# Seven Strassen products for seven pairs of k tiles in each half of a down-projection

## The chip, the cores and the metric

The kernel runs on one core of a Trainium2 chip. Work is shared between TensorE (PE, matrix products), VectorE (DVE) and ScalarE (ACT, both elementwise), GpSimd (POOL, elementwise) and SyncE (SP, which here only starts DMA transfers). The metric is the device time of one execution in microseconds; the kernel before takes 1110.88 us (median of three runs, 1110.84 to 1110.97).

## The reference

One decoder layer on 256 tokens of width 2048. Attention and convolution come first, then the part that matters here, a gated MLP with a three-tap depthwise convolution over the tokens:

```
u = causal_depthwise_conv(rms_norm(x) @ w_up, cw, cb)     # 256 x 11264
a, gate = split(u)                                        # each 256 x 5632
x = x + (silu(gate) * a) @ w_down                         # w_down is 5632 x 2048
return rms_norm(x, final_norm_g)
```

All inputs are float32. TensorE multiplies in the reduced type fp32r, so every operand is split into a high part (a copy in fp32r) and a low part (the value minus its high part), and a product is three matmuls: high times high, high times low, low times high.

## The kernel before, in words

The order of the instructions on each engine is the order in which the program issues them. Weights come in chunks of 128 partitions x 2048 columns (1 MB). `w_dma` starts the transfer of a chunk into one of three raw buffers (`wraw`), `w_split` copies it to a high part `wh` on ScalarE (L110) and subtracts for the low part `wl` on VectorE (L115), three buffers each; the end of the subtraction starts the transfer of the chunk three later. `w_next` hands out a chunk and first splits the chunk two further on. So while TensorE works on chunk c, chunk c+2 is split, into the buffers that chunk c-1 has just left.

The up-projection (L1019, L1021) has 88 chunks. Each of its 22 steps `m` makes two k tiles of the gated activation `gt` (128 x 256 each). `up_out` puts the work behind it in three stages, `join`, `three_taps` and `gate`, and `up_stages` issues the next stage of each waiting step at every chunk. The last of these stages fall into the first chunks of the down-projection.

The down-projection has two halves `h` of 1024 output columns. Each half runs through 22 chunks, called pairs here because one holds two k tiles (256 rows of `w_down`, 1024 columns). For a pair, `down_chunk` multiplies two k tiles x two row blocks `t` (128 tokens) x two column blocks `n` (512 columns), eight products of three matmuls (`mm_rows`, L151 to L153), 24 in all, into four PSUM banks, one for each (t, n). The activations are split four k tiles at a time by `gsplit` (L954 on ScalarE, L955 on VectorE) into `gh` and `gl`, two buffers each, one step of two pairs ahead. The first half's four banks are added to the residual `x2` during the second half (`first_half`). The last two pairs of the second half run in `last_rows`, row block by row block, with the final norm and the output behind them.

Of the kernel before, what the change touches and what calls it, by code (L numbers as in the profile page):

```python
# [35 lines left out]
POOLED = (5, 32)  # L36

# [9 lines left out]
def hybrid_trunk(ctx: ExitStack, tc: tile.TileContext, a: dict, out: bass.AP):  # L47
# [29 lines left out]

    NR, NB, LA = 3, 3, 2
    st = {"dma": 2, "split": 2, "use": 0}
    raws, parts, pieces = {}, {}, []  # L80
    late = []
# [14 lines left out]

    def w_split(cuts):
# [4 lines left out]
        st["split"] += 1  # L102
        n = chunks[c][1]
# [22 lines left out]
    def w_next(cuts=1, ahead=LA):  # L126
        c = st["use"]
        st["use"] += 1
        w_pump()
        while st["split"] <= min(c + ahead, len(chunks) - 1):  # L130
            w_pump()
            w_split(cuts)
# [50 lines left out]
    def norm_evac(src, k, g):  # L183
        nc.scalar.activation(xt_h[:, k], src, AF.Copy, scale=g[:, k:k + 1])
        nc.vector.scalar_tensor_tensor(xt_l[:, k], src, g[:, k:k + 1], xt_h[:, k].bitcast(F32),
                                       op0=OP.mult, op1=OP.subtract)
# [4 lines left out]
    xt = mixp.tile([P, KD, 2, T], F32R, name="xt")  # L191
    xt_h, xt_l = xt[:, :, 0], xt[:, :, 1]
# [3 lines left out]
    with ExitStack() as mx:  # L196
# [40 lines left out]
        for (lo, hi), (xc, *wc) in zip(CUTS, heads):  # L237
            for k in range(lo, hi):
                xk = xc[:, (k - lo) * T:(k - lo + 1) * T]
                nc.scalar.activation(xt_h[:, k], xk, AF.Copy, scale=mix_g[:, k:k + 1])  # L240
                nc.vector.scalar_tensor_tensor(xt_l[:, k], xk, mix_g[:, k:k + 1], xt_h[:, k].bitcast(F32),
# [107 lines left out]
        def tile_chunk(ps, ticks={}):  # L349

            wh, wl = w_next(2)
            for kt in range(KD):
                if kt % 4 == 2:
                    hook(kt // 4, ticks)
                sl = slice(kt * P, (kt + 1) * P)
                mm3(ps, wh[:, sl], wl[:, sl], xt_h[:, kt], xt_l[:, kt], kt == 0, kt == KD - 1)
# [53 lines left out]
        for j in range(8):  # L410
            gb, ab = [b[:, :T] for b in bank[2 * (j if j < 3 else (j + 1) % 2):][:2]]
            if j == 0:
                pair = [w_next(2), w_next(2, 1)]
                for lo, hi in CUTS:
                    for ps, (wh, wl) in zip((gb, ab), pair):
                        for k in range(lo, hi):
                            sl = slice(k * P, (k + 1) * P)
                            mm3(ps, wh[:, sl], wl[:, sl], xt_h[:, k], xt_l[:, k], k == 0, k == KD - 1)
# [195 lines left out]
        for kh in range(2):  # L614
            wh, wl = [w.rearrange("p (k c) -> p k c", c=256) for w in w_next(2)]
            for k in range(8):
# [3 lines left out]
                for t in range(2):  # L620
                    sl = slice(t * P, (t + 1) * P)
                    o = vb[t][:, :256]
                    nc.tensor.matmul(o, xt_h[:, kt, sl], wh[:, k], start=kt == 0, stop=False)
                    nc.tensor.matmul(o, xt_h[:, kt, sl], wl[:, k], start=False, stop=False)
                    nc.tensor.matmul(o, xt_l[:, kt, sl], wh[:, k], start=False, stop=kt == KD - 1)
# [3 lines left out]
        for kq in range(4):  # L629
            wh, wl = [w[:, :4 * 304].rearrange("p (k c) -> p k c", c=304) for w in w_next(2)]  # L630
            for k in range(4):
                kt = kq * 4 + k
                hook(k)
                for t in range(2):
                    sl = slice(t * P, (t + 1) * P)
                    o = vb[t][:, :304]
                    nc.tensor.matmul(o, xt_h[:, kt, sl], wh[:, k], start=kt == 0, stop=False)  # L637
                    nc.tensor.matmul(o, xt_h[:, kt, sl], wl[:, k], start=False, stop=False)
                    nc.tensor.matmul(o, xt_l[:, kt, sl], wh[:, k], start=False, stop=kt == KD - 1)  # L639
# [294 lines left out]
    with ExitStack() as fx:  # L934
        fp = fx.enter_context(tc.tile_pool(name="fp", bufs=1))
        fw = fx.enter_context(tc.tile_pool(name="fw", bufs=2))
        gt = fp.tile([P, NFT, T], F32, name="gt")
# [4 lines left out]
        gq = []  # L942
        gn = {"n": 0}

        def gsplit():
# [3 lines left out]
            if n >= 2 * (NFT // 4):  # L949
                return  # L950
            src = gt[:, 4 * (n % (NFT // 4)):4 * (n % (NFT // 4)) + 4]
            gh = fw.tile([P, 4, T], F32R, name="gh", bufs=2)
            gl = fw.tile([P, 4, T], F32R, name="gl", bufs=2)
            nc.scalar.activation(gh, src, AF.Copy)  # L954
            nc.vector.tensor_sub(gl, src, gh.bitcast(F32))  # L955
            gq.append((gh, gl))

# [4 lines left out]
        def up_out(m, part, banks, ya):  # L962
# [3 lines left out]
            def join():  # L966
                for i in range(2):
                    u = fw.tile([P, T], F32, name="u", bufs=4)
# [5 lines left out]
            def three_taps():  # L974
                for i in range(2):
                    c = part * NFT + 2 * m + i
                    yt = fw.tile([P, T], F32, name="yt", bufs=8)
# [9 lines left out]
            def gate():  # L987
                for i in range(2):
                    nc.scalar.activation(ys[i], ys[i], AF.Silu)
                    nc.vector.tensor_mul(gt[:, 2 * m + i], ys[i], ya[i])  # L990
# [16 lines left out]
        for m in range(NFT // 2):  # L1007
            ya = {}
            if m == NFT // 2 - 1:
                gsplit()  # L1010
            for part in range(2):
                bk = UP_BANKS[2 * ((2 * m + part) % 4):][:2]
                for kh in range(2):
                    wh, wl = [w.rearrange("p (k c) -> p k c", c=256) for w in w_next(1 if m + part + kh else 2)]
                    up_stages()
                    for n, (k, i) in enumerate((k, i) for k in range(8) for i in range(2)):
                        kt = kh * 8 + k
                        sl = slice(i * P, (i + 1) * P)
                        nc.tensor.matmul(bk[i], wh[:, k, sl], xt[:, kt].rearrange("p a t -> p (a t)"),  # L1019
                                         start=kt == 0, stop=False)  # L1020
                        nc.tensor.matmul(bk[i][:, :T], wl[:, k, sl], xt_h[:, kt], start=False, stop=kt == KD - 1)  # L1021
# [9 lines left out]
        def down_chunk(ws, g, banks, k2, t):  # L1031
            sl = slice(t * P, (t + 1) * P)
            for k in range(2):
# [148 lines left out]
```

## Time and profile before

| | us |
|---|---|
| timed runs, median of three | 1110.88 |
| span of the profiled execution, first to last instruction | 1109.3 |
| time of the timed runs outside such a span | 1.6 |
| up-projection | about 363.5 to 853.4 |
| down-projection on TensorE | 853.5 to 1100.9 |
| from there to the end | 8.4 |

Times in the profile count from the first instruction. A row of the timeline gives start, duration, engine, line, operation, tile written and tiles read, count, and in brackets the idle time of the engine ahead of it and what ended it. PE is a matmul on TensorE and PEld a weight load. The end of a matmul in the profile is modelled and overlaps the next one, so the pace is read from starts. A row of a table by stage gives, for a stretch of time, the busy time and the number of instructions of each engine, the granted TensorE clock, the DMA share and GB/s.

### The profile page before, as it was taken

To read this page: it belongs to the slowest core of one execution; us is meant where nothing else is said; L and a number is where in the kernel's file an instruction comes from. 1 tells how busy PE (TensorE), PEld (TensorE's weight loads), DVE (VectorE), ACT (ScalarE), POOL (GpSimd) and SP (SyncE) were. 2 spreads that over 40 slices of the span, in tenths; PEclk is the share of its full clock that TensorE was granted. 3 is DMA by queue.
4 is the path that set the end of the run, shared out by engine and by line. 5 is a ranking of instruction groups with operands and counts; after the bars stand their busy time and mean duration, and the time that the engine had idled before them with its cause. 6 is when DMAs were issued, how large, how long until landed. Compare 5 with 4: busy or idle time off the path is not lost.

```text
span 1109.3 us, 16328 instructions
## 1 busy us (share of the span) xinstructions
PE 1096.5 (99%) x6530; PEld 957.0 (86%) x6530; DVE 768.5 (69%) x1255; ACT 574.3 (52%) x833; POOL 183.7 (17%) x143
## 2 busy tenths in 40 slices
PE   8999999999999999999999999999999999999997
PEld 8999999987788888888888888888888888888885
DVE  7899966776445777777777777777778555556554
ACT  7444456677645545554555455545555444444442
POOL 0878856657000000000000000000000000000000
PEclk9999999999999999999999999999999999999999
DMA  9685526222555555555555555555555555555542
GB/s 375 240 296 188 179 85 232 111 101 91 205 214 184 201 188 189 190 192 188 191 190 192 190 190 189 190 189 189 193 189 193 183 187 190 190 189 190 189 153 77
DMA packets 32425, 207.46 MB, mean 187 GB/s; under 512 B 3883, under 2 KB 6203, under 8 KB 8284
## 3 DMA queue, kind: packets, MB, share of 16 engines
q1 hardware_dynamic: 28972, 199.85, 50.0%
q10 hardware_dynamic: 3376, 6.55, 1.6%
q8 instruction: 51, 0.84, 0.3%
q14 instruction: 26, 0.21, 0.1%
HBM read 204.27 MB, written 2.12 MB: 186 GB/s over the span
## 4 chain that ended last, share of the span: by engine, by line
PE 94%; DVE 2%; ACT 1%; DMA 1%; issue 1%; POOL 0%; SPq 0%; DVEq 0%; POOLq 0%; ACTq 0%
PE bank L1019 29%; PE bank L1021 15%; PE bank L153 10%; PE bank L151 10%; PE bank L152 10%; PE bank L144 5%; PE bank L146 5%; PE bank L145 5%; PE bank L804 1%; PE bank L784 1%; DMA hb<-in_head 1%; DVE wl L115 1%; PE bank L533 0%; PE bank L639 0%; PE bank L637 0%
## 5 line engine op out<-in xcount | busy, mean ns | idle before, releaser
L110 ACT ACTIVATE wh<-wraw 128x2048 fp32r<-128x2048 f32 (+2 forms) x239 | 355.8, 1505 | 369.0 <-issue 153.0
L115 DVE TENSOR_TENSOR wl<-wraw,wh 128x2048 fp32r<-128x2048 f32 (+1 forms) x185 | 363.4, 1970 | 194.8 <-ACT wh L110 194.6
L1019 PE MATMUL bank<-xt,wh 128*128 128x512 f32 x1408 | 488.6, 394 | 0.0
L1021 PE MATMUL bank<-xt,wl 128*128 128x256 f32 x1408 | 390.0, 277 | 0.0
L1019 PEld LDWEIGHTS bank<-xt,wh 128*128 128x128 f32 x1408 | 264.0, 188 | 61.3
L1021 PEld LDWEIGHTS bank<-xt,wl 128*128 128x128 f32 x1408 | 264.2, 188 | 0.0
L144 PE MATMUL bank<-xt,wh 128*128 128x256 f32 x512 | 146.7, 287 | 1.9 <-ACT wh L245 1.9
L146 PE MATMUL bank<-xt,wl 128*128 128x256 f32 x512 | 145.1, 283 | 0.3 <-DVE wl L246 0.2
L145 PE MATMUL bank<-xt,wh 128*128 128x256 f32 x512 | 144.8, 283 | 0.0
L152 PE MATMUL bank<-wl,gh 128*128 128x512 f32 (+1 forms) x360 | 140.8, 391 | 0.0
L151 PE MATMUL bank<-wh,gh 128*128 128x512 f32 (+1 forms) x360 | 140.8, 391 | 0.0
L153 PE MATMUL bank<-wh,gl 128*128 128x512 f32 (+1 forms) x360 | 140.8, 391 | 0.0
L180 POOL TENSOR_TENSOR rstd<-ms,half 128x1 f32<-128x1 f32 x4 | 2.2, 554 | 821.7 <-DVE ms L173 821.7
L115 POOL TENSOR_TENSOR wl<-wraw,wh 128x1024 fp32r<-128x1024 f32 (+1 forms) x54 | 121.4, 2282 | 31.1 <-ACT wh L110 27.5
L144 PEld LDWEIGHTS bank<-xt,wh 128*128 128x128 f32 x512 | 97.7, 191 | 3.7 <-ACT wh L245 2.3
L146 PEld LDWEIGHTS bank<-xt,wl 128*128 128x128 f32 x512 | 97.8, 191 | 0.7 <-DVE wl L246 0.7
L145 PEld LDWEIGHTS bank<-xt,wh 128*128 128x128 f32 x512 | 97.8, 191 | 0.4
L376 DVE SCALAR_TENSOR_TENSOR bank<-us,cw,bank 128x256 f32<-128x256 f32 x232 | 93.9, 481 | 1.7 <-ACT bank L371 1.2
L982 DVE SCALAR_TENSOR_TENSOR yt<-u,vecs,yt 128x255 f32<-128x255 f32 (+1 forms) x176 | 80.9, 480 | 3.1
L151 PEld LDWEIGHTS bank<-wh,gh 128*128 128x128 f32 x360 | 67.8, 188 | 15.8
L153 PEld LDWEIGHTS bank<-wh,gl 128*128 128x128 f32 x360 | 67.8, 188 | 15.8
L152 PEld LDWEIGHTS bank<-wl,gh 128*128 128x128 f32 x360 | 67.8, 188 | 15.8
(182 smaller groups left out, 1030.8 us busy)
## 6 DMA issues: line engine op xcount, KB each, us to landing
wraw<-in_w_u SPq DMA_DIRECT2D x88, 1024.0 KB, 4.7
wraw<-in_w_d SPq DMA_DIRECT2D x44, 1024.0 KB, 4.7
wraw<-in_w_t SPq DMA_DIRECT2D x30, 1024.0 KB, 5.1
wraw<-in_w_o SPq DMA_DIRECT2D x16, 1024.0 KB, 4.8
wraw<-in_w_vg SPq DMA_DIRECT2D x4, 608.0 KB, 3.7
hb<-in_head SPq DMA_DIRECT2D x2, 1024.0 KB, 9.7
xr<-in_x SPq DMA_DIRECT2D x2, 1024.0 KB, 19.0
wb<-rel_scratch ACTq DMA_DIRECT2D x1, 2048.0 KB, 10.3
```

What stands on the lines that cost most here:

```text
L110: nc.scalar.activation(h[:, sl], raw[:, sl], AF.Copy)
L115: (nc.gpsimd if pooled else nc.vector).tensor_sub(l[:, sl], raw[:, sl], h[:, sl].bitcast(F32))
L144: nc.tensor.matmul(ps, wh, xh, start=first, stop=False)
L145: nc.tensor.matmul(ps, wh, xl, start=False, stop=False)
L146: nc.tensor.matmul(ps, wl, xh, start=False, stop=last)
L151: nc.tensor.matmul(ps, xh, wh, start=first, stop=False)
L152: nc.tensor.matmul(ps, xh, wl, start=False, stop=False)
L153: nc.tensor.matmul(ps, xl, wh, start=False, stop=last)
L376: nc.vector.scalar_tensor_tensor(y[:, j] if last else acc[0], us[:, j, k:k + T], cw[:, j, k:k + 1], acc[0], op0=OP.mult, op1=OP.add)
L982: nc.vector.scalar_tensor_tensor(ys[i][:, d:], us_[i][:, :T - d], fcw[:, c, k:k + 1], ys[i][:, d:], op0=OP.mult, op1=OP.add)
L1019: nc.tensor.matmul(bk[i], wh[:, k, sl], xt[:, kt].rearrange("p a t -> p (a t)"), start=kt == 0, stop=False)
L1021: nc.tensor.matmul(bk[i][:, :T], wl[:, k, sl], xt_h[:, kt], start=False, stop=kt == KD - 1)
```

## The change

`SPAIRS` names seven pairs of each half, 6, 8, 10, 12, 14, 16 and 18; they are of kind S, all others are D. In a pair of kind S the 2 x 2 blocks of the activations (two row blocks by two k tiles) and of the weights (two k tiles by two column blocks) are multiplied by Strassen's method in Winograd's form: seven products in place of eight, 21 matmuls in place of 24, into eight banks: the four of the half, and four more that belong to the other half, named 1, 5, 6 and 7.

- Weights: `down_split` splits three of the chunk's four blocks (1536 columns), and makes four sums and differences of blocks in `sums` (one buffer) with three additions on VectorE (1024, 512 and 512 columns). The sums are split too: the high part `xh` on ScalarE at once, the low part `xl` on VectorE at the head of the next chunk's split (`lows`). `xh` and `xl` take the four tiles that held `xt`, the input of the up-projection, which becomes four tiles. The blocks of a chunk are laid out in another order (`SLOT`).
- Activations: `g_sums` makes four sums of the blocks of a pair on GpSimd, right after `gate`, during the up-projection. `sum_split` splits them (512 columns) in the pair ahead, into one buffer each.
- `gsplit` issues only the high part; `g_low` issues the low part at the next odd pair, ahead of that pair's weight split.
- `combine` runs once in each half, after pair 18: one copy from PSUM on ScalarE and eight additions of 512 columns on VectorE, which add the four extra banks into `x2`. These, and the addition of the first half's banks (`first_add`, `first_half`), stand in a list `todo`, of which each pair issues three.
- At the first pair of the down-projection, the remaining up stages are issued all at once, ahead of the first split there, and their buffers are given back to hold `sums`, `gsh` and `gsl`.
- `last_rows` is as before but for the order of blocks.

```diff
+SLOT = {(0, 0): 0, (1, 1): 1, (1, 0): 2, (0, 1): 3}
+SPAIRS = (6, 8, 10, 12, 14, 16, 18)
+KINDS = ["".join("DS"[p in SPAIRS] for p in range(22))] * 2
...
+    def sub_split(hi, lo, src):
+        nc.scalar.activation(hi, src, AF.Copy)
+        return lambda: nc.vector.tensor_sub(lo, src, hi.bitcast(F32))
+
+    def down_split(c):
+
+        for f in lows[:]:
+            f()
+        lows.clear()
+        raw = raws.pop(c)
+        h = wpool.tile([P, CW], F32R, name="wh", bufs=NB)
+        l = wpool.tile([P, CW], F32R, name="wl", bufs=NB)
+        if kinds[c] == "D":
+            parts[c] = (h, l)
+            sub_split(h, l, raw)()
+            w_dma()
+            return
+        xh = mixp.tile([P, CW], F32R, name="xh", tag="xt", bufs=4)
+        xl = mixp.tile([P, CW], F32R, name="xl", tag="xt", bufs=4)
+        parts[c] = (h, l, xh, xl)
+        b, x = [raw[:, i * 512:(i + 1) * 512] for i in range(4)], late_pool[0].tile([P, CW], F32, name="sums", bufs=1)
+        raw_low = sub_split(h[:, :1536], l[:, :1536], raw[:, :1536])
+        nc.vector.tensor_add(x[:, :1024].rearrange("p (a c) -> p a c", a=2),
+                             raw[:, :1024].rearrange("p (a c) -> p a c", a=2), b[3][:, None].to_broadcast([P, 2, 512]))
+        nc.vector.tensor_add(x[:, 1024:1536], x[:, :512], b[1])
+        nc.vector.tensor_add(x[:, 1536:], x[:, 1024:1536], b[2])
+        raw_low()
+        w_dma()
+        lows.append(sub_split(xh, xl, x))
...
-            nc.scalar.activation(gh, src, AF.Copy)
-            nc.vector.tensor_sub(gl, src, gh.bitcast(F32))
+            glows.append(sub_split(gh, gl, src))
             gq.append((gh, gl))
+
+        def g_sums(m):
+
+            if m in SPAIRS:
+                b = gt[:, 2 * m:2 * m + 2].rearrange("p k a t -> p (k a) t")
+                s = gs[:, SPAIRS.index(m)]
+                nc.gpsimd.tensor_sub(s[:, :2], b[:, :1].to_broadcast([P, 2, P]), b[:, 1:3])
+                nc.gpsimd.tensor_sub(s[:, 2], s[:, 1], b[:, 1])
+                nc.gpsimd.tensor_add(s[:, 3], b[:, 3], s[:, 2])
+
+        def sum_split(p):
+            gsh, gsl = [late_pool[0].tile([P, 4, P], F32R, name=n, bufs=1) for n in ("gsh", "gsl")]
+            sub_split(gsh, gsl, gs[:, SPAIRS.index(p)])()
+            sq.append((gsh, gsl))
...
-        def down_chunk(ws, g, banks, k2, t):
...
+        def products(kind, j):
+
+            if kind == "D":
+                return [(names[t, n], 4 * j + 2 * k + 1 - t, SLOT[k, n])
+                        for t in range(2) for k in range(2) for n in range(2)]
+            b = 4 * j
+            return [(2, b + 3, 2), (3, 11, 1), (1, b + 1, 0), (5, 9, 4), (7, 8, 5), (6, 10, 6), (4, b + 2, 7)]
...
+        def down_pair(h, p, g, j, nb):
+
+            kind = KINDS[h][p]
+            if j == 0:
+                gsplit()
+            if not late_pool:
+                while stages:
+                    up_stages()
+                up_only.close()
+                late_pool.append(fx.enter_context(tc.tile_pool(name="fd", bufs=1)))
+            run_todo(3)
+            if j:
+                g_low()
+            if p + 1 in SPAIRS:
+                sum_split(p + 1)
+            ws = w_next()
+            if kind == "S":
+                gsum = sq.pop(0)
+            for name, gi, w in products(kind, j):
+                left[h, name] -= 1
+                wh, wl = [v[:, w % 4 * 512:(w % 4 + 1) * 512] for v in ws[w // 4 * 2:][:2]]
+                xh, xl = [v[:, gi % 8] for v in (g if gi < 8 else gsum)]
+                mm_rows(nb[name], xh, xl, wh, wl, (h, name) not in begun, left[h, name] == 0)
+                begun.add((h, name))
+
+        def combine(h, nb):
...
+                nc.scalar.activation(s["c"], nb[1], AF.Copy)
+
+            add, sub = nc.vector.tensor_add, nc.vector.tensor_sub
+            return [alloc, lambda: add(s["u"], nb[6], s["c"]), lambda: sub(s["v"], s["u"], nb[7]),
+                    lambda: add(x[0, 1], nb[5], x[0, 1]), lambda: add(x[1, 1], nb[5], x[1, 1]),
+                    lambda: add(x[0, 0], x[0, 0], s["c"]), lambda: sub(x[0, 1], x[0, 1], s["u"]),
+                    lambda: add(x[1, 0], x[1, 0], s["v"]), lambda: sub(x[1, 1], x[1, 1], s["v"])]
```

More of the change, by code (lines that the diff above doesn't have):

```diff
@@ L76, in hybrid_trunk @@
             chunks.append((a["w_d"][h, k2], CW))
+    down0 = len(chunks) - NFT
+    kinds = {down0 + i: k for i, k in enumerate(KINDS[0] + KINDS[1])}
     NR, NB, LA = 3, 3, 2
@@ L80, in hybrid_trunk @@
     raws, parts, pieces = {}, {}, []
-    late = []
+    late, lows, late_pool = [], [], []
     clock = {"pe": 0.0, "dve": 0.0}
@@ L102, in w_split @@
         st["split"] += 1
+        if c in kinds:
+            return down_split(c)
         n = chunks[c][1]
@@ L129, in w_next @@
         w_pump()
+        if st["split"] >= len(chunks):
+            for f in lows:
+                f()
+            lows.clear()
         while st["split"] <= min(c + ahead, len(chunks) - 1):
@@ L190, in hybrid_trunk @@
     mixp = ctx.enter_context(tc.tile_pool(name="mix", bufs=1))
-    xt = mixp.tile([P, KD, 2, T], F32R, name="xt")
-    xt_h, xt_l = xt[:, :, 0], xt[:, :, 1]
+    xt = [mixp.tile([P, 4, 2, T], F32R, name="xt", bufs=4) for _ in range(4)]
+    xt_h, xt_l = [[xt[k // 4][:, k % 4, i] for k in range(KD)] for i in range(2)]
     rB = mixp.tile([P, T], F32, name="rB")
@@ L1029, in hybrid_trunk @@
         out_rows = out.rearrange("(t p) d -> p t d", p=P)
-        def down_chunk(ws, g, banks, k2, t):
-            sl = slice(t * P, (t + 1) * P)
-            for k in range(2):
-                kt = 2 * k2 + k
-                for n in range(2):
-                    c = slice(k * 1024 + n * 512, k * 1024 + (n + 1) * 512)
-                    mm_rows(banks[n], g[0][:, kt % 4, sl], g[1][:, kt % 4, sl], ws[0][:, c], ws[1][:, c],
-                            kt == 0, kt == (NFT - 5 if h and n else NFT - 1))
@@ L1040, in first_half, with run_todo @@
-        def first_half(banks, t, n):
+        names = {(0, 0): 2, (0, 1): 3, (1, 0): 4, (1, 1): 8}
+        def products(kind, j):
[4 more added lines that the diff above has]
+            return [(2, b + 3, 2), (3, 11, 1), (1, b + 1, 0), (5, 9, 4), (7, 8, 5), (6, 10, 6), (4, b + 2, 7)]
+        def run_todo(n):
+            for _ in range(min(n, len(todo))):
+                todo.pop(0)()
```

125 lines of the change are left out of this document (77 added, 48 removed).

## The prediction

> **What bounds the kernel now.** I read the page's busy shares and chain first.
>
> ```profile
> span 1109.3 us, 16328 instructions
> ...
> PE 1096.5 (99%) x6530; PEld 957.0 (86%) x6530; DVE 768.5 (69%) x1255; ACT 574.3 (52%) x833; POOL 183.7 (17%) x143
> ...
> PE 94%; DVE 2%; ACT 1%; DMA 1%; issue 1%; POOL 0%; SPq 0%; DVEq 0%; POOLq 0%; ACTq 0%
> ```
>
> TensorE is busy 99% of the span and holds 94% of the chain. VectorE is busy 69%, but that is an average, so the stage that the change touches is read by itself: the table by stage, with the down-projection on TensorE and the tail behind it.
>
> ```profile
> 853.50:1100.90 247.40, 247.40 (x1082) 199.95 (x1080) 138.17 (x100) 108.43 (x88) 0.55 (x1) 1.00 0.48 172
> ...
> 1100.90:1109.30 8.40, 0.16 (x2) 0.00 (x0) 2.17 (x5) 1.84 (x4) 0.55 (x1) 0.69 0.51 193
> ```
>
> In the down-projection TensorE is busy all 247.40 us at the full clock (1.00), VectorE 138.17 us (56%) and ScalarE 108.43 us (44%). So a matmul taken away there is worth its full spacing, as long as the others keep up. The spacing is read from the two engines behind it, in a quiet part; first the first matmul of the stage and the counts of one of its three lines, then ScalarE over two pairs and VectorE in the first of them.
>
> ```profile
> 853.49 0.39 PE L151 MATMUL bank<-wh,gh 128*128 128x512 f32 x1
> ```
> ```profile
> L152 PE MATMUL bank<-wl,gh 128*128 128x512 f32 x344 | 136.4, 396 | 0.0
> L152 PE MATMUL bank<-wl,gh 128*128 128x256 f32 x16 | 4.5, 280 | 0.0
> ```
> ```profile
> 977.16 1.06 ACT L954 ACTIVATE gh<-gt 128x1024 fp32r<-128x1024 f32 x1 [3.47 <-PE bank L152]
> 978.12 1.90 ACT L110 ACTIVATE wh<-wraw 128x2048 fp32r<-128x2048 f32 x1
> 983.01 1.92 ACT L110 ACTIVATE wh<-wraw 128x2048 fp32r<-128x2048 f32 x1 [2.99 <-PE bank L153]
> 988.40 1.06 ACT L954 ACTIVATE gh<-gt 128x1024 fp32r<-128x1024 f32 x1 [3.48 <-PE bank L152]
> ```
> ```profile
> 978.25 1.22 DVE L955 TENSOR_TENSOR gl<-gt,gh 128x1024 fp32r<-128x1024 f32 x1 [2.24 <-ACT gh L954]
> 980.06 2.29 DVE L115 TENSOR_TENSOR wl<-wraw,wh 128x2048 fp32r<-128x2048 f32 x1 [0.59 <-ACT wh L110]
> ```
>
> The `gh` copy of ScalarE waits for the last matmul of the step before, so 977.16 and 988.40 are two pairs apart: 11.24 us for 48 matmuls, 0.2342 us each (the 0.39 us of the first row is a modelled duration and overlaps the next matmul). Check: three lines have 1032 matmuls of 512 columns and 48 of 256 (half as long each) make 1056 x 0.2342 = 247.3 us, the 247.40 of the table. A pair of 24 takes 5.62 us, and pair 22 starts at 853.49 + 22 x 5.62 = 977.1. VectorE is done with the even pair's split at 980.06 + 2.29 = 982.35, 5.2 us into the pair, and that chunk is wanted 11.24 us into it: a lead of 6 us.
>
> The Trainium skill ("TensorE: Matmul & The Clock Gate", section "Wait — 56ns, not 53.3ns?") has 215.7 ns for such a matmul at the full clock; by it the saving below would be 42 x 0.2157 = 9.1 us. No stretch of this stage runs at that pace, so the row decides.
>
> **TensorE's part.** Each S pair has 21 matmuls in place of 24, all of 128x512: 14 pairs x 3 = 42 fewer, 42 x 0.2342 = **9.84 us**. An S pair takes 21 x 0.2342 = 4.92 us, an S and a D pair together 45 x 0.2342 = 10.54 us. Nothing is added on TensorE: each product goes to another bank than the one before it, but that holds before the change too (`down_chunk` changes bank after every three matmuls).
>
> **VectorE's part**, the one that could take it back. The prices, from the groups by shape, VectorE then ScalarE:
>
> ```profile
> L115 DVE TENSOR_TENSOR wl<-wraw,wh 128x2048 fp32r<-128x2048 f32 x129 | 295.7, 2292 | 178.6 <-ACT wh L110 178.6
> L955 DVE TENSOR_TENSOR gl<-gt,gh 128x1024 fp32r<-128x1024 f32 x22 | 26.9, 1225 | 40.3 <-ACT gh L954 40.3
> L469 DVE TENSOR_TENSOR y<-y,bank 128x1024 f32<-128x1024 f32 x4 | 4.8, 1217 | 0.9 <-PE bank L449 0.9
> L1044 DVE TENSOR_TENSOR x<-x,gfin 128x512 f32<-128x512 f32 x4 | 2.8, 692 | 3.3 <-ACT sq L1043 3.3
> L246 DVE TENSOR_TENSOR wl<-hb,wh 128x512 fp32r<-128x512 f32 x4 | 2.6, 686 | 0.0
> ```
> ```profile
> L110 ACT ACTIVATE wh<-wraw 128x2048 fp32r<-128x2048 f32 x129 | 246.8, 1913 | 284.5 <-issue 130.5 <-PE bank L1019 109.8 <-PE bank L153 44.2
> L954 ACT ACTIVATE gh<-gt 128x1024 fp32r<-128x1024 f32 x22 | 23.3, 1059 | 65.8 <-PE bank L152 65.8
> L245 ACT ACTIVATE wh<-hb 128x512 fp32r<-128x512 f32 x4 | 2.3, 614 | 0.0
> ```
>
> VectorE costs 0.69 us for 512 columns, 1.22 for 1024 and 2.29 for 2048, with a broadcast operand in PSUM as well (L469); so 1.76 for 1536 (midway). ScalarE: 0.61, 1.06, 1.91, so 1.48. Per S and D pair VectorE now has eight operations: three additions (1.22 + 0.69 + 0.69), the raw low part (1.76), `gl` (1.22), the low part of the activations' sums (0.69), `xl` (2.29), and the D chunk's low part (2.29): 10.85 us of durations. Before, two pairs cost 2 x 2.29 + 1.22 = 5.80 of 11.24. The operations overlap a little, as the start of the stage shows:
>
> ```profile
> 852.19 1.91 DVE L982 SCALAR_TENSOR_TENSOR yt<-u,vecs,yt 128x255 f32<-128x255 f32 x4
> 855.53 2.29 DVE L115 TENSOR_TENSOR wl<-wraw,wh 128x2048 fp32r<-128x2048 f32 x1 [0.29 <-ACT wh L110]
> 857.74 0.42 DVE L970 TENSOR_TENSOR u<-bank,u 128x256 f32<-128x256 f32 x1
> 858.19 0.42 DVE L971 TENSOR_TENSOR u<-u,rB 128x256 f32<-128x256 f32 x1
> ```
>
> An operation that depends on nothing new starts 0.08 before the end of the one ahead of it (855.53 + 2.29 = 857.82, the next at 857.74); one that reads the last result starts 0.03 after it (858.16, 858.19). Six of the eight are of the first kind, two additions of the second: 10.85 - 6 x 0.08 + 2 x 0.03 = **10.43 us of 10.54**. VectorE is 99% full in this stretch, yet not over.
>
> Whether TensorE waits is read from due times. From s, the start of an S pair p, in the steady state: ScalarE's `gh` 0 to 1.0 and high part (1536) 0.9 to 2.4; VectorE's raw low part for pair p+2 2.4 to 4.2, `gl` to 5.3, `gsl` to 6.0, `xl` 5.9 to 8.2, the low part of chunk p+3 8.1 to 10.4, then the next additions, to 12.9, which is 10.54 + 2.4 again: it closes. ScalarE has 1.06 + 1.48 + 1.91 + 0.61 + 1.91 = 7.0 of 10.54 and no late step: `gsh` waits for the sixth product of the pair ahead, 0.7 before the odd pair starts. Wanted: `gl` at 10.54 + 2 x 0.234 = 11.0 (margin 5.7); `gsl` in the second product, 11.7 (5.7); `xl` in the fourth, at 10.54 + 10 x 0.234 = 12.9 (**4.7**); chunk p+3 at 15.7 (5.3). So TensorE waits for nothing. The one wait that is new on VectorE is `gsl` for `gsh`, with `xl` and the D chunk's low part queued behind it; both are in the schedule. The cover is thin in load and thick in margin: without it, each us per period that VectorE is late costs one after the 4.7 are used up.
>
> The Trainium skill ("VectorE: DVE Perf Modes", section "The DRAIN you can't avoid") speaks against this: the next VectorE operation would start only when the pipe is empty. By it the load is the full 10.85, 0.31 over; six periods make 1.9 us, still under 4.7. The rows above show the 0.08 of overlap against it.
>
> **What else moves.** Banks and tiles: the extra banks of the first half are those that the last up steps leave at the start (wanted in pair 6), those of the second are drained by pair 23 (wanted in pair 28), and `combine` has read its banks by pair 20, where the second half takes them in 22; `xt` is free at 853.5 and first written in pair 4. Cost 0. The transfers: the same 44 of 1 MB, each started when its raw buffer is free.
>
> ```profile
> wraw<-in_w_d SPq DMA_DIRECT2D x44, 1024.0 KB, 4.7
> ```
>
> The D chunk's buffer is freed at s + 10.4, the new chunk lands 4.7 later, at 15.1, and is first read by the additions at about 20.8. Nothing is due earlier on SP's queue; cost 0, and even a transfer of 10 us would be covered.
>
> GpSimd's 21 sums fall in the up-projection, where its queue is empty; the nearest row is
>
> ```profile
> L115 POOL TENSOR_TENSOR wl<-wraw,wh 128x608 fp32r<-128x608 f32 x8 | 11.8, 1520 | 6.0 <-ACT wh L110 6.0
> ```
>
> 1.52 us for 608 columns, so under 1 us each, wanted tens of us later: 0. The gate product written through a reversed view keeps its 256 columns: 0.
>
> The start of the stage: all three last stages now stand ahead of the split of chunk 2. ScalarE before:
>
> ```profile
> 853.57 1.92 ACT L110 ACTIVATE wh<-wraw 128x2048 fp32r<-128x2048 f32 x1 [1.70 <-PE bank L1019]
> 855.40 0.64 ACT L969 ACTIVATE u<-bank 128x256 f32<-128x256 f32 x2
> 861.18 1.08 ACT L978 ACTIVATE yt<-u,vecs 128x256 f32<-128x256 f32 x2
> 867.48 0.71 ACT L989 ACTIVATE yt<-yt 128x256 f32<-128x256 f32 x2
> ```
>
> With s = 853.5: the copies `u` 0.1 to 0.7; VectorE, free at 854.1 (852.19 + 1.91), add and multiply twice, 0.6 to 2.2; `yt` to 2.8; four taps (1.91) to 4.05; Silu to 4.5; the high part (1.91) 4.4 to 6.3, the low part to 8.6, wanted at 11.5; then `gl`, to 9.8, wanted at 11.7. Margin **1.9 us**: cost 0. If every step of this chain took a third longer, TensorE would wait about 1 us, once. What stands behind it on VectorE, chunk 3's low part, ends at 12.0 and is wanted at 17.1.
>
> `combine` and the first half's additions: eight of 0.69 (5.5 us) over pairs 19 to 21 and as many over 22 to 24, all of them D, where VectorE has 5.4 us free in every two pairs: 0. The second half's `combine` leaves six additions and two older ones (eight of 0.61 from start to start) to the last two pairs. VectorE before, there:
>
> ```profile
> 1089.85 0.69 DVE L1078 TENSOR_TENSOR x<-bank,x 128x512 f32<-128x512 f32 x1 [0.78 <-PE bank L153]
> 1092.66 0.69 DVE L1060 TENSOR_TENSOR x<-bank,x 128x512 f32<-128x512 f32 x1 [2.12 <-PE bank L153]
> 1094.07 0.42 DVE L1060 TENSOR_TENSOR x<-bank,x 128x256 f32<-128x256 f32 x1 [0.72 <-PE bank L153]
> 1095.48 0.42 DVE L1060 TENSOR_TENSOR x<-bank,x 128x256 f32<-128x256 f32 x1 [0.35 <-PE bank L153]
> 1098.84 0.68 DVE L1060 TENSOR_TENSOR x<-bank,x 128x512 f32<-128x512 f32 x1
> 1099.69 0.42 DVE L1060 TENSOR_TENSOR x<-bank,x 128x256 f32<-128x256 f32 x1 [0.17 <-PE bank L153]
> 1101.10 0.42 DVE L1060 TENSOR_TENSOR x<-bank,x 128x256 f32<-128x256 f32 x1 [0.35 <-PE bank L153]
> ```
>
> By the reckoning above the last chunk's low part ends 0.7 us ahead of pair 20, and the eight end 4.2 into it, where the first addition of the last rows began about 3 in before (1092.66, with the pair at 1089.6): 1.1 us late. The idle stretches behind it (0.72, 0.35, 0.17, 0.35) add up to 1.59. So between 0 and 0.5 us at the end; I take **0.1**.
>
> **Sum.** The profiled span 1109.3 becomes 1109.3 - 9.84 + 0.1 = 1099.6; the timed runs lie 1.6 above their span, so 1110.88 - 9.74 = 1101.1. I forecast **1101.1 us**, a ratio of 1.009.
>
> **Rivals.**
>
> 1. *VectorE late, part of the gain lost.* The price of the additions with two SBUF operands and a sum read right after its writing is inferred, and 99% leaves nothing. At 10% more the period is 11.47, 0.93 late each; six periods after the first make 5.6, less the 4.7 margin 0.9 us per half: 1102.9. At 15%: 1.45 x 6 - 4.7 = 4.0 per half, 1109.1. Against it: all rows of one size agree within 1%, whatever the operands. Chance 0.13.
> 2. *The start or the tail late*: the 1.9 us margin lost through slower handovers, or `combine` not absorbed: 1102 to 1104. Chance 0.07.
> 3. *Slower.* The same VectorE bound past its turning point, as one mechanism: TensorE loses 4.92 us per half where 6 x (period - 10.54) - 4.7 exceeds 4.92, a period of 12.14, that is 16% over 10.43. At 20% the period is 12.52, the loss 7.2 per half, 1101.1 + 14.4 = 1115.5. For it: a stage whose waits pass ScalarE twice per chunk with one `sums` buffer could fail to overlap, so that the 7.0 us of ScalarE add in part to VectorE's. Against it: in the schedule above only the raw low part waits for ScalarE. Chance 0.07.
> 4. *The change does not shorten TensorE*: if spacing came from something per pair (handover of buffers), fewer matmuls would not help. For it there is nothing: the idle time of TensorE at pair borders is none. About 1110.9, chance 0.03.
>
> **How the numbers follow.** The forecast has a chance of 0.70 with its own range, 1100.7 to 1101.8 (tail 0 to 0.5, spacing 0.2342 plus or minus 1% and 0.2 for the runs). The range that leaves out no more than two in ten adds rival 2 and the milder part of rival 1, to 12%: 1100.5 to 1105.0. Faster by over 0.2% (2.2 us, about what a measurement of this kernel can tell) means under 1108.7: the forecast, rival 2 and most of rival 1, 0.70 + 0.07 + 0.11 = 0.88. Within 0.2%: 0.01 of rival 1 and rival 4, 0.04. Slower: rival 3 and what is left, 0.08.
>
> **What would show it.** TensorE: 1038 rows of `wh` by high part in place of 1080 over all three lines together, and a stage of 247.4 - 9.8 = 237.6 us with no idle rows. VectorE: busy near 99% in the stretch of pairs 4 to 18, additions of 1.22 and 0.69, `xl` ending more than 4 us ahead of its first matmul. The forecast is wrong if TensorE rows of S pairs wait for `xl`, `gl` or `wl`; if the period of an S and a D pair is over 10.6 us; or if the last matmul still lies 8.4 us ahead of the end but starts later than 1091.

## The result and the profile after

The changed kernel takes **1100.58 us** (median of four runs, 1100.47 to 1100.82) where the kernel before, beside it, takes 1110.9: a ratio of 0.9906, with a 95% interval of 0.9895 to 0.9918. The forecast was 1101.1 with a range of 1100.5 to 1105.0. The gain was forecast as 9.7 us and is 10.3 us, and the time lies at the very low end of the range. By the ratio, 1110.88 x 0.9906 = 1100.44, it is just below. So the direction and the mechanism held, but one term was sized too small and the range had no room on that side. Most of what follows asks which term it was.

The page's span, busy shares and chain, after:

```profile
span 1099.0 us, 16381 instructions
...
PE 1088.0 (99%) x6488; PEld 951.2 (87%) x6488; DVE 846.1 (77%) x1341; ACT 602.2 (55%) x863; POOL 196.3 (18%) x164
...
PE 95%; DVE 2%; ACT 1%; issue 1%; DMA 0%; POOL 0%; DVEq 0%; POOLq 0%; ACTq 0%
```

TensorE still bounds the kernel, with 42 matmuls fewer (6530 to 6488). The table by stage, again with the down-projection on TensorE first and the tail second:

```profile
853.59:1090.70 237.11, 237.11 (x1040) 191.90 (x1038) 211.07 (x186) 136.26 (x118) 0.55 (x1) 1.00 0.51 180
1090.70:1099.00 8.30, 0.08 (x1) 0.00 (x0) 2.17 (x5) 1.84 (x4) 0.55 (x1) 0.82 0.49 186
```

TensorE is busy through the whole stage at the full granted clock (1.00). VectorE went from 138 to 211 us in a stage that is shorter. The starts of TensorE's rows give the lengths: the first and the last matmul of the stage, and between them the first matmul of pair 16 (kind S), of pair 17 (D) and of pair 18 (S), and pair 18's first use of `xl`.

```profile
853.59 0.39 PE L193 MATMUL bank<-wh,gh 128*128 128x512 f32 x1
...
939.84 0.40 PE L193 MATMUL bank<-wh,gh 128*128 128x512 f32 x1
...
944.71 0.40 PE L193 MATMUL bank<-wh,gh 128*128 128x512 f32 x1
...
950.34 0.40 PE L193 MATMUL bank<-wh,gh 128*128 128x512 f32 x1
...
952.65 0.40 PE L194 MATMUL bank<-xl,gsh 128*128 128x512 f32 x1
...
1090.50 0.28 PE L195 MATMUL bank<-wh,gl 128*128 128x256 f32 x1
```

From first to last start the stage has 236.91 us; before, from 853.49 to 1100.79, it had 247.30. From the last matmul to the end there are 8.5 us in both. So all of the gain is in the stage, **10.39 us**. The D pair takes 950.34 - 944.71 = 5.63 us, as before (5.62 to 5.63). The S pair takes 944.71 - 939.84 = 4.87 us, where the prediction had 4.92.

VectorE from the additions made in pair 14 to the last step of those made in pair 16, one whole period and the next:

```profile
929.10 1.22 DVE L125 TENSOR_TENSOR sums<-wraw 128x1024 f32<-128x1024 f32 x1
...
939.60 1.22 DVE L125 TENSOR_TENSOR sums<-wraw 128x1024 f32<-128x1024 f32 x1
940.85 0.69 DVE L127 TENSOR_TENSOR sums<-sums,wraw 128x512 f32<-128x512 f32 x1
941.57 0.69 DVE L128 TENSOR_TENSOR sums<-sums,wraw 128x512 f32<-128x512 f32 x1
942.28 1.76 DVE L105 TENSOR_TENSOR wl<-wraw,wh 128x1536 fp32r<-128x1536 f32 x1
943.96 1.22 DVE L105 TENSOR_TENSOR gl<-gt,gh 128x1024 fp32r<-128x1024 f32 x1
945.09 0.68 DVE L105 TENSOR_TENSOR gsl<-gs,gsh 128x512 fp32r<-128x512 f32 x1
945.69 2.29 DVE L105 TENSOR_TENSOR xl<-sums,xh 128x2048 fp32r<-128x2048 f32 x1
947.89 2.28 DVE L105 TENSOR_TENSOR wl<-wraw,wh 128x2048 fp32r<-128x2048 f32 x1
```

The eight operations follow each other with hardly a gap. The period is 10.50 us, which is TensorE's (950.34 - 939.84). `xl` ends at 947.98 and is first wanted at 952.65: a margin of **4.67 us**, against 4.7 forecast. ScalarE in the same period, whose order matters for the second experiment:

```profile
939.80 1.06 ACT L104 ACTIVATE gh<-gt 128x1024 fp32r<-128x1024 f32 x1 [3.76 <-PE bank L194]
940.77 1.48 ACT L104 ACTIVATE wh<-wraw 128x1536 fp32r<-128x1536 f32 x1
942.29 1.92 ACT L104 ACTIVATE xh<-sums 128x2048 fp32r<-128x2048 f32 x1
944.12 0.61 ACT L104 ACTIVATE gsh<-gs 128x512 fp32r<-128x512 f32 x1
944.64 1.90 ACT L104 ACTIVATE wh<-wraw 128x2048 fp32r<-128x2048 f32 x1
```

### The profile page after: what moved, and what is told of

Its sections match the earlier page's. It is cut to its first block, busy times and chain, and to the rows that moved or that the text cites. A ratio compares the mean times of both kernels' runs of the same rounds, so it can differ in the third digit from the quotient of the medians.

```text
span 1099.0 us, 16381 instructions
## 1 busy us (share of the span) xinstructions
PE 1088.0 (99%) x6488; PEld 951.2 (87%) x6488; DVE 846.1 (77%) x1341; ACT 602.2 (55%) x863; POOL 196.3 (18%) x164
## 4 chain that ended last, share of the span: by engine, by line
PE 95%; DVE 2%; ACT 1%; issue 1%; DMA 0%; POOL 0%; DVEq 0%; POOLq 0%; ACTq 0%
PE bank L1085 30%; PE bank L1087 15%; PE bank L194 10%; PE bank L193 10%; PE bank L195 10%; PE bank L186 5%; PE bank L188 5%; PE bank L187 5%; PE bank L846 1%; PE bank L826 1%; DVE wl L153 1%; PE bank L575 0%; PE bank L681 0%; PE bank L679 0%; PE bank L680 0%
## 5 line engine op out<-in xcount | busy, mean ns | idle before, releaser
L148 ACT ACTIVATE wh<-wraw 128x1024 fp32r<-128x1024 f32 (+2 forms) x195 | 271.8, 1414 | 300.5 <-issue 133.2
L153 DVE TENSOR_TENSOR wl<-wraw,wh 128x2048 fp32r<-128x2048 f32 (+1 forms) x141 | 262.9, 1872 | 131.2 <-ACT wh L148 130.9
L105 DVE TENSOR_TENSOR wl<-wraw,wh 128x2048 fp32r<-128x2048 f32 (+1 forms) x44 | 93.2, 2118 | 22.2 <-ACT wh L104 21.9
L194 PE MATMUL bank<-wl,gh 128*128 128x512 f32 (+1 forms) x276 | 107.6, 390 | 0.0
L193 PE MATMUL bank<-wh,gh 128*128 128x512 f32 (+1 forms) x276 | 107.5, 390 | 0.0
L195 PE MATMUL bank<-wh,gl 128*128 128x512 f32 (+1 forms) x276 | 107.4, 389 | 0.0
L104 ACT ACTIVATE wh<-wraw 128x2048 fp32r<-128x2048 f32 (+1 forms) x44 | 77.8, 1769 | 16.6 <-PE bank L195 9.2
L1008 POOL TENSOR_TENSOR gs<-gt 128x256 f32<-128x256 f32 x7 | 5.2, 737 | 421.7 <-DVE gt L1054 421.7
```

The lines of the kernel that those rows point to most:

```text
L105: return lambda: nc.vector.tensor_sub(lo, src, hi.bitcast(F32))
L148: nc.scalar.activation(h[:, sl], raw[:, sl], AF.Copy)
L153: (nc.gpsimd if pooled else nc.vector).tensor_sub(l[:, sl], raw[:, sl], h[:, sl].bitcast(F32))
L193: nc.tensor.matmul(ps, xh, wh, start=first, stop=False)
L194: nc.tensor.matmul(ps, xh, wl, start=False, stop=False)
L195: nc.tensor.matmul(ps, xl, wh, start=False, stop=last)
```

## The experiments

The kernel without S pairs was timed ten times and the one with eight of them four times; all others were timed once. The kernel before spread over 0.6 us beside them (1110.75 to 1111.36), so smaller differences are read from the lengths of pairs in the traces, and not from the times.

**All pairs of kind D.** Everything of the change stays but the method itself.

```diff
-SPAIRS = (6, 8, 10, 12, 14, 16, 18)
+SPAIRS = ()
...
```

> No pair is of kind S; every other edit of the change stays (block order of the chunks, up stages issued at once, low parts of the rows ahead of the split, xt in four tiles). If the gain comes from the 42 matmuls alone, TensorE's stage is back at 247.4 us and the time at 1110.9, plus or minus 0.5. If the other edits carry part of the gain (the 0.5 us above the forecast, or more), the time is 1110.4 or less. If they cost something that the matmuls had to make good, it is 1111.4 or more.

Measured 1111.14 us (1110.89 to 1112.82), a ratio of 1.0003 (0.9994 to 1.0013) to the kernel before. The split in another order, the four tiles of `xt`, the late up stages issued together and the moved `gl` are worth nothing by themselves. The whole gain comes with the S pairs.

**The low part of the activations at once, not queued ahead of the next weight split.** This undoes the third point in the list of the change.

```diff
-            glows.append(sub_split(gh, gl, src))
+            sub_split(gh, gl, src)()
```

> The low part of the rows is issued right behind its high part, at the even pair ahead of the additions, as before the change, and not at the odd pair. VectorE then waits there for the copy on ScalarE, with the additions queued behind. By the due times VectorE runs about 1 us later in each pair and the margin of xl falls from 4.7 to about 3.6 us: TensorE still waits for nothing and the time stays at 1100.6, plus or minus 0.4. If VectorE sets the pace of this stretch, its idle 1 us per period comes out at TensorE: 12 us in 12 periods, 1112.

Measured 1104.82 us: 4.2 us of the gain are gone, which neither expectation had. VectorE in one period, from its last addition to the next group, and ScalarE's two rows beside it:

```profile
936.73 0.69 DVE L128 TENSOR_TENSOR sums<-sums,wraw 128x512 f32<-128x512 f32 x1
937.34 1.75 DVE L105 TENSOR_TENSOR wl<-wraw,wh 128x1536 fp32r<-128x1536 f32 x1
939.92 0.69 DVE L105 TENSOR_TENSOR gsl<-gs,gsh 128x512 fp32r<-128x512 f32 x1 [0.83 <-ACT gsh L104]
...
944.94 1.22 DVE L105 TENSOR_TENSOR gl<-gt,gh 128x1024 fp32r<-128x1024 f32 x1
946.07 1.22 DVE L125 TENSOR_TENSOR sums<-wraw 128x1024 f32<-128x1024 f32 x1
```
```profile
937.45 1.92 ACT L104 ACTIVATE xh<-sums 128x2048 fp32r<-128x2048 f32 x1 [4.76 <-DVE sums L128]
939.28 0.61 ACT L104 ACTIVATE gsh<-gs 128x512 fp32r<-128x512 f32 x1
```

`gl` costs the same 1.22 us, but stands ahead of the additions now. ScalarE's `xh` needs the last addition (L128), and `gsh` stands behind `xh` on ScalarE: 2.44 us from 937.45 to the end of `gsh` at 939.89. VectorE's next step that waits for it, `gsl`, has only the raw low part in front, which ends at 939.09, so VectorE idles **0.83 us** in every period. In the changed kernel `gl` stands just there (943.96 to 945.18, with `gsh` done at 944.73) and covers it. The period is 11.32 us in place of 10.50.

The margin of `xl` also starts lower, at 3.31 us in pair 6 where the changed kernel has 5.45. In pair 4 the additions for pair 6 stand behind `gl`, which waits for `gh` on ScalarE, and that copy for a matmul of TensorE; so they start at 878.13 us and not at 874.81 as in the changed kernel:

```profile
876.99 1.23 DVE L105 TENSOR_TENSOR gl<-gt,gh 128x1024 fp32r<-128x1024 f32 x1 [2.24 <-ACT gh L104]
878.13 1.22 DVE L125 TENSOR_TENSOR sums<-wraw 128x1024 f32<-128x1024 f32 x1
```

From 3.31 the margin falls by 0.83 a period and is used up in pair 14; pairs 14, 16 and 18 take 5.02, 5.69 and 5.70 us in place of 4.87. That is 1.8 us in each half, 3.6 of the 4.2; another 0.5 us stand behind the last matmul, in the tail, where VectorE comes late. The loss needs both parts: six periods of 0.83 are 5.0 us, which a starting margin of 5.45 would have covered (an estimate; no run has only one of the two).

**VectorE more loaded.** The first addition is made twice, then three times.

```diff
-        nc.vector.tensor_add(x[:, :1024]..., raw[:, :1024]..., b[3]...)
+        for _ in range(2):                                  # 3 in the second kernel
+            nc.vector.tensor_add(x[:, :1024]..., raw[:, :1024]..., b[3]...)
```

> The first addition of each weight sum (1024 columns) is done twice, so VectorE has 1.14 us more per period of an S and a D pair: 10.41 + 1.14 = 11.55 against the 10.50 that TensorE takes. By the due times VectorE falls 1.05 us further behind in each of six periods, 6.3 us, of which 4.7 are covered: TensorE waits 1.6 us in each half, in the last S pairs, for xl; 1100.6 + 3.2 = 1103.8 (1102 to 1106). If VectorE already sets the pace, all 14 x 1.05 = 14.7 us come out: 1115. If it has more room than reckoned: 1100.6.

> The first addition is done three times: 2.28 us more, 12.69 per period, 2.19 over TensorE's 10.50. By the due times 6 x 2.19 - 4.7 = 8.4 us per half, 1100.6 + 16.9 = 1117.5 (1114 to 1121), slower than the kernel before: past the turning point reckoned at 16% more load. With VectorE setting the pace throughout: 1100.6 + 14 x 2.19 = 1131. With more room than reckoned: under 1111.

Measured **1104.77** us with one more and **1122.87** with two, so 6.1 us faster and 12.0 us slower than before. Two successive groups of additions with one more, and with two:

```profile
932.97 2.47 DVE L126 TENSOR_TENSOR sums<-wraw 128x1024 f32<-128x1024 f32 x2
...
944.62 2.48 DVE L126 TENSOR_TENSOR sums<-wraw 128x1024 f32<-128x1024 f32 x2
```
```profile
926.69 3.74 DVE L126 TENSOR_TENSOR sums<-wraw 128x1024 f32<-128x1024 f32 x3
...
939.62 3.74 DVE L126 TENSOR_TENSOR sums<-wraw 128x1024 f32<-128x1024 f32 x3
```

An addition that writes the tile that the one ahead has just written adds 1.25 us from start to start (2.47 - 1.22 in the first row), not 1.14: it does not overlap. So the periods are 11.65 and 12.92 us. With one more, the margin of `xl` falls, 5.3, 4.1, 3.0, 1.8, 0.7 us in pairs 6 to 14, and is used up in pair 16; pairs 16 and 18 take 5.52 and 6.04 us. With two more it starts at 4.04 us and is used up in pair 10, and the later S pairs take 7.3. What TensorE waits for there, by the list of waits of the second kernel:

```profile
PE bank L195 <- DVE xl L105: 6.8, 10, 0.7
PE bank L196 <- DVE gl L105: 5.1, 8, 0.6
PE bank L195 <- DVE wl L105: 2.4, 8, 0.3
```

The prediction's reckoning for a late VectorE, six periods' lateness less the margin, twice, gives 1101.1 + 2 x (6 x (11.65 - 10.54) - 4.7) = 1105.0 and 1101.1 + 2 x (6 x 2.38 - 4.7) = 1120.3. It is right to 0.3 us for the first, in part by luck: its 1101.1 is 0.5 too high, the margin starts at 5.3 us and not at 4.7, and the tail, 0.5 longer here, is not in it. It is 2.6 too low for the second: there the margin starts at 4.04 us, which is 1.3 us over two halves, and the tail is 0.5 longer; the rest is not broken down. A straight line between the two runs passes the time before at a period of 12.1 us; the turning point was put at 12.14.

**One S pair more in each half.** Pair 4 joins them; the scratch `sq3`, of which 512 columns are used, is cut to make room.

```diff
-SPAIRS = (6, 8, 10, 12, 14, 16, 18)
+SPAIRS = (4, 6, 8, 10, 12, 14, 16, 18)
...
-        sq3 = fp.tile([P, 1024], mybir.dt.bfloat16, name="sq3")
+        sq3 = fp.tile([P, 512], mybir.dt.bfloat16, name="sq3")
```

> Pair 4 of each half is of kind S as well, eight in place of seven. By the price of an S pair in the trace (5.62 - 4.87 = 0.75 us) two more bring 1.5 us: 1099.1. VectorE's load in the two pairs added is the same as in the others, and the first half's additions fall into pairs 0 to 2 of the second, ahead of its additions for pair 4, 1.2 us: margins of xl of 4.6 us in the first half and about 3.4 in the second, no wait on TensorE. If VectorE at the start of a half has no room beside the up stages or those additions, TensorE waits there and the time is 1100.6 or more.

Measured **1099.05** us (1099.0 to 1099.08), a ratio of 0.9892 (0.9875 to 0.9908) to the kernel before: 1.5 us under the changed kernel, 2 x 0.75 for two more S pairs. It is the fastest of all. In its second half VectorE starts late and shows its own pace:

```profile
1047.65 1.22 DVE L125 TENSOR_TENSOR sums<-wraw 128x1024 f32<-128x1024 f32 x1
...
1058.05 1.22 DVE L125 TENSOR_TENSOR sums<-wraw 128x1024 f32<-128x1024 f32 x1
```

10.40 us for the eight operations, under TensorE's 10.50, and so the margin of `xl` grows there, from 2.3 us in the first S pair (3.4 were expected) by 0.10 a period to 3.0.

**The low part of the sums on GpSimd**, which has nothing to do in this stage, to take 2.2 us per period off VectorE.

```diff
-        lows.append(sub_split(xh, xl, x))
+        nc.scalar.activation(xh, x, AF.Copy)
+        lows.append(lambda: nc.gpsimd.tensor_sub(xl, x, xh.bitcast(F32)))
```

> The low part of the weight sums goes from VectorE to GpSimd, which has nothing else to do in this stage. VectorE loses 2.2 us per period (8.2 of 10.5 left), GpSimd takes some 4.6 us for 2048 columns (2.15 ns a column, from its rows of 608 and 1024 columns). If TensorE waits for nothing in the changed kernel, relieving VectorE brings nothing: 1100.6, plus or minus 0.4; xl ends about 9 us into the period, a margin near 3.9. If the two engines hold each other up over two operands in SBUF, VectorE's rows beside GpSimd's get longer; held up for all of GpSimd's 4.6 us, VectorE needs 12.8 per period and the time is about 1118.

Measured 1122.68 us, 11.7 us slower than before. The groups of `xl` and `gsl` in the down-projection, and one of each in order of time:

```profile
L132 POOL TENSOR_TENSOR xl<-sums,xh 128x2048 fp32r<-128x2048 f32 x14 | 73.4, 5241 | 212.2 <-ACT xh L131 204.8 <-PE bank L196 7.4
L105 DVE TENSOR_TENSOR gsl<-gs,gsh 128x512 fp32r<-128x512 f32 x14 | 71.6, 5113 | 0.0
```
```profile
880.50 5.54 POOL L132 TENSOR_TENSOR xl<-sums,xh 128x2048 fp32r<-128x2048 f32 x1 [74.98 <-ACT xh L131]
...
881.46 5.13 DVE L105 TENSOR_TENSOR gsl<-gs,gsh 128x512 fp32r<-128x512 f32 x1
```

`gsl` is the same 512 columns that cost 0.68 us in the changed kernel, and takes 5.13: it ends 0.55 us after GpSimd's subtraction, which began before it. VectorE wins 2.2 us and loses 4.4, its period is 12.6 us, and TensorE waits for `gsl` (15.2 us in ten waits). The time is 4.7 us above the 1118 that were expected for this case: `gsl` is wanted in the second product of an S pair, had 5.7 us of margin and now ends 4.4 us later, which leaves 1.3 us of cover where the expectation counted on the 4.7 of `xl` (an estimate). The Trainium skill ("SBUF — State Buffer", section "Who interferes with whom") says that a VectorE instruction with two SBUF inputs contends with a GpSimd one that reads SBUF, and that the ports they share are an exclusive lock; these rows agree.

**Why an S pair takes 4.87 us and not 4.92.** Eight kernels separate what could make the difference. From the trace's starts in ns, an S pair of the changed kernel has 4874 from its first matmul to the next pair's (4889 to 4892 in the first S pair of a half), 232 per matmul; 21 matmuls of plain blocks have 4920, 234 per matmul.

The order of a D pair's products, (row block, k tile, column block) before, in two other orders:

```diff
-                        for t in range(2) for k in range(2) for n in range(2)]
+                        for k in range(2) for t in range(2) for n in range(2)]   # first kernel
+                        for k in range(2) for n in range(2) for t in range(2)]   # second kernel
```

> The eight products of a D pair run k tile by k tile: first the four banks, then the four again, so three products lie between two on one bank in place of one; neighbouring products still share their stationary rows. The 0.55 us by which the change gained more than 42 x 0.2342 lie in the S pairs, 4.874 us for 21 matmuls, 0.2321 each, against 0.2343 in D pairs. If the distance between two uses of a bank makes that difference, a D pair falls from 5.62 to 5.57 and the time, with 28 D pairs left, by 1.5 us to 1099.1. If it is that an S pair never loads the same rows twice in succession, D pairs stay at 5.62 and the time at 1100.6.

> As the run before it, but with the row block as the innermost loop: neighbouring products share the weight block that streams through and have different stationary rows, and three products lie between two on one bank. If either the distance between uses of a bank or the repeated rows make the 0.002 us per matmul, D pairs take 5.57 us and the kernel 1099.1; if it is the weight block read twice in a pair, 5.62 or more and 1100.6.

Measured 1100.81 and 1100.67 us, with D pairs of 5.62 and S pairs of 4.87 us in both. So how often the same block is loaded twice in a row, or which bank follows which, does not matter here.

No S pairs, but the eighth product left out of the same 14 pairs:

```diff
-SPAIRS = (6, 8, 10, 12, 14, 16, 18)
+SPAIRS = ()
+SEVEN = (6, 8, 10, 12, 14, 16, 18)
...
-                        for t in range(2) for k in range(2) for n in range(2)]
+                        for t in range(2) for k in range(2) for n in range(2)][:7 if short else 8]
```

> No pair is of kind S, but the same 14 pairs leave out their eighth product (the output lacks it): 21 matmuls of plain blocks by plain blocks, no sums, no combine, VectorE far from full. What is asked is why a matmul of an S pair takes 0.2322 us and not the 0.2342 of a D pair. If it is what is read (sums, xh, xl) or the banks that are written, such a pair takes 21 x 0.2342 = 4.92 us and the kernel 1111.1 - 14 x 0.705 = 1101.2 us; if it is the number of matmuls in a pair, 4.876 us and 1100.6.

S pairs with the four banks of the half only:

```diff
-            return [(2, b + 3, 2), (3, 11, 1), (1, b + 1, 0), (5, 9, 4), (7, 8, 5), (6, 10, 6), (4, b + 2, 7)]
+            return [(2, b + 3, 2), (3, 11, 1), (8, b + 1, 0), (4, 9, 4), (2, 8, 5), (3, 10, 6), (4, b + 2, 7)]
...
-                    if KINDS[h].rfind("S") == p:
-                        todo.extend(combine(h, nb))
```

> The changed kernel with the seven products of an S pair added into the four banks of the half, no two in a row into one bank, and without the combine (so the output is not the sum that the method needs). If the shorter spacing in S pairs comes from the four further banks, an S pair takes 4.92 us and the kernel about 1101.2; if from the operands or the count, 4.876 and 1100.6. The combine itself was put at 0, the tail at 0 to 0.1: nothing more is expected of its absence.

Seven plain products take 4.92 us (1101.21 us in all); S products into four banks take 4.87 (1100.69). So it is neither the count nor the banks, but what is read. The two operands apart:

```diff
+            return [..., (3, b, 1), ..., (5, b + 3, 4), (7, b, 5), (6, b + 1, 6), ...]      # plain activations
+            return [..., (3, 11, 1), ..., (5, 9, 2), (7, 8, 1), (6, 10, 0), (4, b + 2, 2)]  # plain weights
```

> In S pairs the four products that read the activations' sums gsh and gsl read plain blocks of gh and gl instead (the output is not the reference's); the weights' sums xh and xl are read as before, and all other engines do the same work. If the activations' sums (the operand that TensorE loads as weights) make the shorter spacing, an S pair now takes 4.92 us and the kernel about 1101.2; if the weights' sums (the operand that it streams) make it, 4.876 and 1100.6; if both, between.

> The counterpart: the four products that read the weights' sums xh and xl read blocks of wh and wl instead (the output is not the reference's); gsh and gsl are read as before, and all other engines do the same work. If the weights' sums make the shorter spacing, an S pair takes 4.92 us and the kernel about 1101.2; if the activations' sums make it, 4.876 and 1100.6; if both, between.

Measured 1101.52 and 1100.84 us. The first matmuls of pairs 16, 17 and 18 with plain activations:

```profile
940.14 0.39 PE L193 MATMUL bank<-wh,gh 128*128 128x512 f32 x1
...
945.06 0.39 PE L193 MATMUL bank<-wh,gh 128*128 128x512 f32 x1
...
950.68 0.39 PE L193 MATMUL bank<-wh,gh 128*128 128x512 f32 x1
```

945.06 - 940.14 = 4.92 us: with `gh` and `gl` alone the S pair has the pace of a D pair. With plain weights and `gsh`, `gsl` it keeps 4.87. So the shorter spacing comes with the operand that TensorE loads, not with the one that it streams. Last, whether the values or the place of these tiles make it:

```diff
-                nc.gpsimd.tensor_sub(s[:, :2], b[:, :1].to_broadcast([P, 2, P]), b[:, 1:3])   # and two more sums
+                nc.gpsimd.tensor_copy(s[:, :2], b[:, 1:3])                                    # and two more copies
```
```diff
-            gsh, gsl = [late_pool[0].tile([P, 4, P], F32R, name=n, bufs=1) for n in ("gsh", "gsl")]
+            gsh = late_pool[0].tile([P, 5, P], F32R, name="gsh", bufs=1)[:, 1:]
+            gsl = late_pool[0].tile([P, 4, P], F32R, name="gsl", bufs=1)
...
-        sq3 = fp.tile([P, 1024], mybir.dt.bfloat16, name="sq3")
+        sq3 = fp.tile([P, 512], mybir.dt.bfloat16, name="sq3")
```

> GpSimd writes copies of plain blocks where the activations' sums stood (the output is not the reference's): TensorE loads the same tiles gsh and gsl from the same places, with the values of plain blocks. If the shorter spacing comes from the values, an S pair takes 4.92 us and the kernel about 1101.2; if from where gsh and gsl lie or how they alternate with gh and gl, 4.876 and 1100.6.

> gsh starts one block of 128 columns further on in a tile made one block longer, so that gsh lies elsewhere and its distance to gsl is another; nothing else changes. If the place in SBUF sets the spacing, the length of an S pair changes from 4.876 us (to up to 4.92, or below 4.87); if any tile apart from gh and gl does it, it stays at 4.876 within 0.005.

Measured 1100.65 and 1100.59 us, both with S pairs of 4874 to 4875 ns. The values do not matter, and neither does a shift by one block. What is left is that two further tiles are loaded in turn with `gh` and `gl`. The number of tiles alone does not explain it: earlier in the kernel before, the same three lines load two other tiles in turn, `ma_h` and `ma_l`, and 24 matmuls take 299.41 - 293.81 = 5.60 us there, 233.3 ns each (other work runs beside them).

```profile
293.81 0.39 PE L151 MATMUL bank<-wh,ma_h 128*128 128x512 f32 x1
...
299.41 0.39 PE L151 MATMUL bank<-wh,ma_h 128*128 128x512 f32 x1
```

Why `gsh` and `gsl` save 2 ns per matmul stays open: no run here moved them far from where they lie, or spread the loads of a D pair over more tiles.

## Why the prediction was right, and where it was wrong

**What bounds the kernel**: right. TensorE held the chain before and after, the stage stayed without idle time, and matmuls taken away there came off the end.

**TensorE's part: here it failed.** The count was right: 42 fewer, 1038 rows of the three lines of `mm_rows`. The price was not: "42 x 0.2342 = 9.84" takes it that the 294 matmuls that stay in S pairs cost what they cost in D pairs. They cost 0.2321 us, so an S pair saves 5.624 - 4.875 = 0.75 us and not 3 x 0.2342 = 0.70, over 14 pairs 10.5 us. The stage shows 10.39. With 10.4 the prediction's own sum gives 1110.88 - 10.4 + 0.1 = 1100.6, the measured time. The **range** failed with it: "spacing 0.2342 plus or minus 1%" was applied to the 42 matmuls that go, which is 0.1 us, although the 294 that stay read other tiles; 1% of 294 x 0.2342 is 0.7 us, and the measured difference is 0.6. The low end should have been near 1100.0.

**VectorE's part**: right. 10.43 us were forecast for the eight operations and 10.40 are measured where VectorE runs behind (the second half with eight S pairs); in the changed kernel it is held to TensorE's 10.50. The additions cost 1.22 and 0.69, the 1536 columns 1.76, as taken. The 10.85 us that the prediction worked out by the Trainium skill ("VectorE: DVE Perf Modes", section "The DRAIN you can't avoid") is not what these rows show. The same section says that an operation that is not held back starts earlier, and these rows agree: `gsl` starts at 945.09, ahead of the end of `gl` at 945.18.

**The due times**: right to 0.1 us. With s = 939.84, the raw low part runs 2.4 to 4.2, `gl` to 5.3, `gsl` to 5.9, `xl` to 8.1, the D chunk's low part to 10.3. The margin of `xl` is 4.67 (4.7), and that of `gl`, done at 945.18 and wanted by pair 18's third matmul at 950.80, 5.6 (5.7).

**"The one wait that is new on VectorE is `gsl` for `gsh`"**: right, but the prediction did not say what covers it. It is `gl`, and its place. With `gl` ahead of the additions VectorE idles 0.83 us in every period and starts the additions of each half some 3.3 us later, and together that costs 4.2 us. That ScalarE, at 7.0 of 10.54 us, has no late step holds only for the changed order. The part of the change that looked like a detail of margins holds four tenths of the gain.

**The start**: right. ScalarE's high part of chunk 2 began 4.4 us into the stage, and `gl` ended at 9.8, as forecast. ScalarE's row, VectorE's two, and the matmul that wants `gl`:

```profile
858.03 3.71 ACT L104 ACTIVATE wh<-wraw 128x2048 fp32r<-128x2048 f32 x2
```
```profile
859.96 2.29 DVE L105 TENSOR_TENSOR wl<-wraw,wh 128x2048 fp32r<-128x2048 f32 x1 [1.38 <-ACT wh L104]
862.17 1.22 DVE L105 TENSOR_TENSOR gl<-gt,gh 128x1024 fp32r<-128x1024 f32 x1
```
```profile
865.30 0.39 PE L195 MATMUL bank<-wh,gl 128*128 128x512 f32 x1
```

862.17 + 1.22 = 863.39, 1.9 us ahead of 865.30: the forecast margin.

**The tail**: 0.1 was taken, 0 measured (8.5 us behind the last matmul both times). VectorE: the last two of the eight additions (L1203), the first additions of the last rows behind them (L1176), and the first one that is in time again:

```profile
1082.17 1.28 DVE L1203 TENSOR_TENSOR x<-bank,x 128x512 f32<-128x512 f32 x2
1083.37 1.01 DVE L1176 TENSOR_TENSOR x<-bank,x 128x512 f32<-128x512 f32 x2
...
1085.19 0.42 DVE L1176 TENSOR_TENSOR x<-bank,x 128x256 f32<-128x256 f32 x1
```

Counted back from the last matmul, the last two pairs start 11.2 us earlier, at 1079.3. The first addition starts 4.1 us into them (forecast 4.2, before 3.1), the third 5.9 as before: the idle time took up the lateness before it reached the end.

**The rivals.** VectorE late, and slower past a turning point: neither came, but the two loaded kernels bear out the mechanism and its turning point (12.14 us forecast, 12.1 between the runs), though the starting margins were 5.3 and 4.0 us and not 4.7. By that line the changed kernel stands 1.7 us per period away from being slower than before. The start and the tail were not late. Nor did the fourth come: fewer matmuls did help. The spacing depends on something besides the count, but on what is loaded and not on the pair, and here it added to the gain.

## What to carry to other kernels

A price read in one place holds for the operands of that place: when a change keeps most of a group and gives it other operands, put the uncertainty on those that stay, not only on those that go. Where an engine is 99% full but has margin, look for the operation that covers each wait for another engine; its place in the queue can be worth as much as its duration (moving `gl`, of 1.22 us, cost 4.2 us here, and so did one more addition of 1.25). Before work is moved to an idle engine, test whether the two can run at once: if they cannot, one stands still while the other works, as `gsl` did for 4.4 us.

## What was not expected of the hardware

- TensorE's spacing depends on the tiles that the loaded operand comes from: 232 ns per 128x512 matmul where `gsh`, `gsl`, `gh` and `gl` take turns, 234 ns with `gh` and `gl` alone, 233.3 with `ma_h` and `ma_l` in an earlier stage. Values, order, banks, the streamed operand and a shift by one block did not change it; the cause is open.
- A VectorE subtraction of 512 columns with both operands in SBUF takes 5.1 us in place of 0.68 when a GpSimd subtraction of 2048 columns runs.
- An operation of VectorE that overwrites the tile of the one ahead of it costs 1.25 us where an independent one of 1.22 us adds 1.14.
